# First modulation of a two-layer diffusion backbone: float32 products on four column groups, with tokens and context loaded first

## The chip, the cores and the metric

The kernel runs on one core of a Trainium2 chip. The metric is the device time of one execution in microseconds (us); lower is better. TensorE (PE) multiplies, ScalarE (ACT) and VectorE (DVE) work on elements, GpSimd (POOL) fills constants, and SyncE (SP) issues every transfer from device memory (HBM).

## The reference, cut to what matters

256 latent tokens `x` and 256 context tokens `ctx`, 2048 features each, pass two layers in float32. Ahead of each layer a conditioning vector gives shift, scale and gate vectors. The change concerns the first two of them (`sh1`, `sc1`) of layer 0, for tokens and context, and the first use of them, the queries' and keys' latents.

```python
for l in range(DEPTH):
    mod_x = (jax.nn.silu(c) @ w_mod[l] + b_mod[l])[:, None, :]      # c: (1, 2048), w_mod[l]: (2048, 12288)
    sh1, sc1, g1, sh2, sc2, g2 = jnp.split(mod_x, 6, axis=-1)
    hx = modulate(rmsnorm(x, norm1[l]), sh1, sc1)                   # h * (1 + scale) + shift
    if need_ctx:                                                    # layer 0
        mod_c = jax.nn.silu(c_ctx) @ w_mod[l] + b_mod[l]
        csh1, csc1, ... = jnp.split(mod_c, 6, axis=-1)
        hc = modulate(rmsnorm(ctx, norm1[l]), csh1, csc1)
    ...                                                             # layer 0: attention and pooling of
    x = x + g1 * yx                                                 # hx @ w_in, hc @ w_in; layer 1: Fourier
    x = x + g2 * sq_relu_mlp(modulate(rmsnorm(x, norm2[l]), sh2, sc2), w_mlp1[l], w_mlp2[l])
return rmsnorm(x, final_norm)
```

## The kernel before, in words

Features lie on the 128 partitions, in 16 blocks; tokens lie along the free axis. Weights come as tiles `W` of 128 x 2048 float32 (1 MB each) into a pool of seven buffers. `split` turns part of a tile into two float32r halves, H (a rounded copy, by ACT) and L (the rest, by DVE), and a product is then H times the activation's two halves plus L times its first.

The order on SP and PE is the order of the program text; DVE, ACT and POOL are ordered by the scheduler. A load waits for its buffer, and so for the last reader of the tile that held it. The other modulation vectors of both layers are products on DVE (`mod_step`), which are paced between later loads.

The stage that the change touches is the first one. `w_mod`'s shift and scale columns of layer 0 are 32 tiles: four groups `ng` of 512 features, for each first the scale (`which` 1) and then the shift (0), each in four tiles `kt`. A tile holds four blocks `kb` of 128 inputs by 512 features. `start_tile` multiplies it with the two conditioning vectors (tokens, context): a stationary operand of few useful columns, and the 512 features of the tile streaming past it, into a row tile `mrow` of one PSUM bank. The number `PLAIN[ng]` says how many of the four blocks are multiplied as float32 as they are (`cstf`, 32 stationary columns), and the others are split (`cst`, 128 columns of which four are used: the H and the L part of each vector). A float32 product is one instruction in the program and two passes on PE in the trace.

When the four tiles of a row are done, and one tile of the next row is through, `start_columns` copies the row to SBUF (ACT) and turns it into columns with four small products with `sel` (`mtr`), and DVE adds the bias. `latents(ng)` then loads `w_kv` and `w_q` for these four blocks of 128 features, makes `hc` and `hx` (`modulated`: DVE writes `xr`, ACT the first half of `h`, DVE the second), and does two half steps of products into the banks `ka` and `qa`. Its first half follows tile `LT[0]` of the next group's eight and its second half tile `LT[1]`, both counted from 0; the second half of the third group's and all of the fourth's come after the last tile. The tokens `x` are loaded after tile `LX` (5), the context `cx` after tile 7, and their sums of squares and the two normalizing rows follow at the tiles `NT` (8 and 9).

After this stage come pooling woven with attention (first products into `pu`), the output projection, the MLP, and layer 1.

Of the kernel before, what the change touches and what calls it, by code (L numbers as in the profile page):

```python
# [16 lines left out]
P = 128  # L17
# [10 lines left out]
WINDOWS = (2, 4, 8, 16)  # L28
PLAIN = (2, 1, 1, 0)
LATE = 2  # L30
LX, LC, NT, LT = 5, (7,), (8, 9), (2, 5)

# columns of the packed vectors
V_N1 = (0, 16)
# [10 lines left out]
def hybrid_dit(ctx: ExitStack, tc: tile.TileContext, xT, ctxT, c2, cb_in, vecs, wmod_s, wmod0, wmod1,  # L45
               w_q, w_kv, w_pl, w_uq, w_ukv, w_pool, w_oe, w_oo, w1, w2,
               rope, band, ident_in, sel_in, dftc, dftn, out):
    nc = tc.nc
    # the tensor engine and the loads go in the order of this text
    ctx.enter_context(tc.manual_schedule(engines={mybir.EngineType.SP, mybir.EngineType.PE}))  # L50
# [32 lines left out]

# [1 line left out]
    todo = []  # L85
# [26 lines left out]

# [1 line left out]
    def load(src, n=2048):  # L114
# [8 lines left out]
    def split(w, lo, n, nn):  # L123
        """n columns from lo of a tile, as [(H, L)] by row blocks of nn"""
        h = hp.tile([P, 1024], F32R, name="H", tag="H")
        l = hp.tile([P, 1024], F32R, name="L", tag="L")
        nc.scalar.copy(h[:, :n], w[:, lo:lo + n])  # L127
        nc.vector.tensor_tensor(l[:, :n], w[:, lo:lo + n], h.bitcast(F32)[:, :n], ALU.subtract)  # L128
        return [(h[:, i:i + nn], l[:, i:i + nn]) for i in range(0, n, nn)]
# [9 lines left out]
    def wide(ps, wts, j, acts, first, last):  # L139
        """a block of 128 output features in a bank: [HH | HL + LH]"""  # L140
        js = slice(j * P, (j + 1) * P)
        n = len(wts)
        for k, (h, l) in enumerate(wts):
            mm(ps, h[:, js], acts[k], first and k == 0, False)
            mm(ps[:, T:], l[:, js], acts[k][:, :T], False, last and k == n - 1)

    def narrow(o, wts, j, acts, first, last):
        """the same, summed in half a bank; first starts the bank"""
        js = slice(j * P, (j + 1) * P)
        n = len(wts)  # L150
        for k, (h, l) in enumerate(wts):
            mm(o, h[:, js], acts[k][:, :T], first and k == 0, False)
            mm(o, h[:, js], acts[k][:, T:], False, False)
            mm(o, l[:, js], acts[k][:, :T], False, last and k == n - 1)

    def plain(o, wts, j, acts, first, last):
        """the same in float32 as it is, for products too small to repay the splitting"""
        js = slice(j * P, (j + 1) * P)
# [4 lines left out]
    def linear(tiles, acts, evac, nb=4, slim=False, drain=False):  # L163
        """nb output blocks from [(sources of their tiles of four row blocks, first row block)];
        yields after each half of a tile; with drain the last tile goes block by block"""
        if slim:
# [4 lines left out]
        for i, (srcs, k0) in enumerate(tiles):  # L171
            for s, src in enumerate(srcs):
                w = load(src)
                final = i == len(tiles) - 1
                for k in (0, 2):
# [9 lines left out]
                    for j in range(4):  # L185
# [3 lines left out]
                        else:  # L189
                            wide(o, wts, j, part, first, last)  # L190
                        # a bank is read only when all of it is done
                        if last and not slim:
# [10 lines left out]
    def weave(main, filler):  # L203
        """main says how many steps of the filler come before its next one"""
        for n in main:
# [3 lines left out]

# [1 line left out]
    def sumsq(acc, src, first):  # L211
# [7 lines left out]
    def token_sums(ps, src, n, first, last, nb=2):  # L219
        """adds a block's sums over its features, by token, in columns of 128"""  # L220
        for b in range(nb):
            mm(ps[:, b:b + 1], src[:, b * P:(b + 1) * P], ones[n], first and b == 0, last and b == nb - 1)

    def rstd(ps, nb=2, first=False):
        """1/sqrt(mean + eps) by token"""
        v, s, r, a = (tiny(4, m)[:, :nb] for m in ("va", "sd", "rr", "nw"))
# [17 lines left out]
    def spread(r, nb=2):  # L244
        """those columns as rows, the same on each partition"""
        o = bank("rb")
# [14 lines left out]
    def scales(m, which, norm, lo=0, n=NB):  # L261
        """norm * (1 + scale), in place of the scale"""
        v = m[:, which, lo:lo + n]
# [6 lines left out]

# [1 line left out]
    c2s = cp.tile([P, 32], F32, name="c2s")  # L272
# [19 lines left out]

# [1 line left out]
    csil = cp.tile([P, 2, NB], F32, name="csil")  # L294
# [4 lines left out]
    nc.vector.tensor_copy(cstf[:, :, 1], csil[:, 1])  # L299
    cst = [ap.tile([P, 4, P], F32R, name=f"cst{i}", tag="a") for i in range(4)]  # L300
    for i in range(4):
        nc.gpsimd.memset(cst[i].bitcast(F32), 0.0)
        for s in range(2):
            nc.scalar.copy(cst[i][:, :, s], csil[:, s, 4 * i:4 * i + 4])
            nc.vector.tensor_tensor(cst[i][:, :, 2 + s], csil[:, s, 4 * i:4 * i + 4],
                                    cst[i].bitcast(F32)[:, :, s], ALU.subtract)

    def start_tile(row, ng, which, kt):
        """a tile's share of 512 features of shift (0) or scale (1), for the tokens and the context"""
        w = load(wmod_s[which * 4 + ng, kt])  # L310
        whole_ = PLAIN[ng]
        for lo in range(0, 4 - whole_, 2):
            n = min(2, 4 - whole_ - lo)
            for i, (h, l) in enumerate(split(w, lo * 512, n * 512, 512)):
                kb = lo + i
                mm(row, cst[kt][:, kb, :], h, kt == 0 and kb == 0, False)
                mm(row, cst[kt][:, kb, :], l, False, kt == 3 and kb == 3)
        for kb in range(4 - whole_, 4):
            mm(row[:32], cstf[:, 4 * kt + kb, :], w[:, kb * 512:(kb + 1) * 512], False, kt == 3 and kb == 3)

# [12 lines left out]

# [1 line left out]
    qa = [bank(f"qa{i}") for i in range(2)]  # L335
# [3 lines left out]
    def latents(ng):  # L339
# [5 lines left out]
        for i in range(2):  # L345
# [14 lines left out]
            yield  # L360

    columns = lat = None
    for ng in range(4):
        for which in (1, 0):
            row = bank("mrow")
            for kt in range(4):
                start_tile(row, ng, which, kt)
                if ng == 0 and which == 1 and kt == 0:
                    nc.sync.dma_start(vec, vecs)
                    nc.sync.dma_start(sel, sel_in)  # L370
                    nc.sync.dma_start(ident, ident_in)
                at = 8 * ng + 4 * (1 - which) + kt
                if at == LX:
                    for i in range(4):
                        nc.sync.dma_start(x[:, 4 * i:4 * i + 4], xT[:, 4 * i:4 * i + 4])
                    accs = [stat("accx"), stat("accc")]
                    for i in range(NB):
                        sumsq(accs[0], x[:, i], i == 0)
                if at in LC:
                    for i in range(8 // len(LC)):  # L380
                        cx.append(funit("cx").rearrange("p (a b) -> p a b", b=T))
                        i = len(cx) - 1
                        nc.sync.dma_start(cx[i], ctxT[:, 2 * i:2 * i + 2])
                        for i in (2 * i, 2 * i + 1):
                            sumsq(accs[1], cx[i // 2][:, i % 2], i == 0)
                if columns and kt == 0:
# [32 lines left out]

# [1 line left out]
    mixed = []  # L421

    def residual(l, which, stats, slim=False):
        """adds gate * product to the stream (and gathers its squares)"""
        def at(ng):
# [20 lines left out]
    def pooling():  # L446
        # by token, so that the centred means are products with a banded matrix
        us = [[bank(f"pu{tb}{hf}") for hf in range(2)] for tb in range(2)]
# [45 lines left out]

# [1 line left out]
    attn = []  # L496

    def rotary(s):
        """in place on [2 x 64, tokens]"""
        r = scr("rot")  # L500
# [5 lines left out]
    def attention():  # L506
# [35 lines left out]
        def project(pr):  # L542
            """a pair's heads: queries and keys by feature, values by token"""
            w = load(w_ukv[pr], 1024)
# [142 lines left out]

# [1 line left out]
    wc = load(dftc)  # L689
# [12 lines left out]
    def channels(g):  # L702
        """cosine and sine sums over a group's channels, by token"""
        st = []
# [22 lines left out]
    def positions(st):  # L727
        """the same over the tokens, by feature: blocks k, 128 + k and their mirrors"""
        def part(o, lo, which, first):
# [53 lines left out]
def _pack(w, nn=512, nk=4):  # L783
    """[K, N] in tiles [N / nn, K / (128 nk)] of [128, nk * nn], one run per partition"""
    k, n = w.shape
# [4 lines left out]
def _tables():  # L790
# [21 lines left out]
    sel = np.zeros((P, 2))  # L812
    sel[:4] = [[1, 0], [0, 1], [1, 0], [0, 1]]
    return [np.ascontiguousarray(t, dtype=np.float32) for t in (rope, band, np.eye(P), sel, dftc, dftn)]
# [51 lines left out]
```

## Time and profile before

| | |
|---|---|
| median of 3 runs | 2037.41 us (2036.52 to 2053.14) |
| span of the profiled execution | 2038.8 us |
| PE busy | 1993.2 us (98%) |
| DVE busy | 1508.1 us (74%) |
| ACT busy | 1067.7 us (52%) |
| moved from and to HBM | 537.68 MB, mean 264 GB/s |

The span runs from the first to the last instruction of one profiled execution. No separate time of that execution is listed beside its span, which lies 1.4 us above the median of the runs. Busy shares are means over stages with different limits, so the first stage is read by itself.

### The profile page before, as it was taken

To read this page: it belongs to the slowest core of one execution; us is meant where nothing else is said; L and a number is where in the kernel's file an instruction comes from. 1 tells how busy PE (TensorE), PEld (TensorE's weight loads), DVE (VectorE), ACT (ScalarE), POOL (GpSimd) and SP (SyncE) were. 2 spreads that over 40 slices of the span, in tenths; PEclk is the share of its full clock that TensorE was granted. 3 is DMA by queue.
4 is the path that set the end of the run, shared out by engine and by line. 5 is a ranking of instruction groups with operands and counts; after the bars stand their busy time and mean duration, and the time that the engine had idled before them with its cause. 6 is when DMAs were issued, how large, how long until landed. Compare 5 with 4: busy or idle time off the path is not lost.

```text
span 2038.8 us, 29093 instructions
## 1 busy us (share of the span) xinstructions
PE 1993.2 (98%) x11492; PEld 1712.8 (84%) x11492; DVE 1508.1 (74%) x2084; ACT 1067.7 (52%) x1715; POOL 2.9 (0%) x14
## 2 busy tenths in 40 slices
PE   6999999999999999999999999999999999999997
PEld 2678778988888888888888888888888888888887
DVE  5877868989888788888878677798555655655564
ACT  5564545355544554554555455556455545645563
POOL 0000000000000000000000000000000000000000
PEclk9999999989999999999999999999999999999998
DMA  9777888959988888887888516599555555555541
GB/s 387 266 303 297 328 305 321 374 180 392 343 330 331 328 310 327 318 321 295 344 319 325 217 62 230 183 347 375 189 190 196 181 194 188 184 199 194 186 145 42
DMA packets 77465, 537.68 MB, mean 264 GB/s; under 512 B 8848, under 2 KB 9104, under 8 KB 13968
## 3 DMA queue, kind: packets, MB, share of 16 engines
q1 hardware_dynamic: 77328, 535.82, 71.0%
q8 instruction: 90, 1.47, 0.3%
q14 instruction: 47, 0.39, 0.1%
HBM read 533.69 MB, written 2.10 MB: 263 GB/s over the span
## 4 chain that ended last, share of the span: by engine, by line
PE 96%; DMA 1%; DVE 1%; ACT 1%; issue 0%; SPq 0%; DVEq 0%; ACTq 0%
PE mm L82 80%; PE mrow L82 3%; PE pu L82 2%; PE ka L82 2%; PE sc L82 2%; DMA W<-in_wmod_s 1%; PE qa L82 1%; PE f L82 1%; PE pv L82 1%; PE qn L82 1%; PE v L82 1%; PE p L82 1%; PE kn L82 1%; PE rb L82 0%; PE var L82 0%; PE tr L607 0%
## 5 line engine op out<-in xcount | busy, mean ns | idle before, releaser
L128 DVE TENSOR_TENSOR L<-W,H 128x1024 fp32r<-128x1024 f32 (+2 forms) x668 | 795.4, 1207 | 390.6 <-ACT H L127 387.7
L127 ACT CAST H<-W 128x1024 fp32r<-128x1024 f32 (+2 forms) x668 | 685.5, 1037 | 605.1 <-PE mm L82 531.7
L82 PE MATMUL mm<-h,H 128*128 128x512 f32 x2048 | 720.7, 396 | 3.6 <-DVE h L258 3.6
L82 PE MATMUL mm<-hid,H 128*128 128x512 f32 (+1 forms) x2176 | 718.4, 382 | 0.0
L82 PE MATMUL mm<-h,L 128*128 128x256 f32 x2048 | 575.8, 281 | 0.0
L82 PE MATMUL mm<-hid,L 128*128 128x256 f32 x2048 | 574.6, 281 | 0.0
L82 PEld LDWEIGHTS mm<-hid,H 128*128 128x128 f32 x2176 | 399.8, 188 | 84.5
L82 PEld LDWEIGHTS mm<-h,H 128*128 128x128 f32 x2048 | 385.7, 188 | 94.7 <-issue 2.1
L82 PEld LDWEIGHTS mm<-h,L 128*128 128x128 f32 x2048 | 388.7, 190 | 0.0
L82 PEld LDWEIGHTS mm<-hid,L 128*128 128x128 f32 x2048 | 387.4, 189 | 0.0
L98 DVE SCALAR_TENSOR_TENSOR W<-W,cb 128x2048 f32<-128x2048 f32 x160 | 365.0, 2284 | 0.0
L433 DVE SCALAR_TENSOR_TENSOR x<-mm,mods,x 128x256 f32<-128x256 f32 x176 | 79.9, 479 | 43.8 <-PE mm L82 26.4
L82 PE MATMUL mm<-fr,H 128*128 128x512 f32 (+1 forms) x320 | 91.0, 352 | 0.0
L432 ACT ACTIVATE rt<-mm,mods 128x256 f32<-128x256 f32 x132 | 61.7, 469 | 52.4 <-PE mm L82 50.9
L666 ACT ACTIVATE rl<-g 128x256 f32<-128x256 f32 x128 | 53.2, 415 | 53.9 <-DVE g L664 53.3
L82 PE MATMUL mm<-fr,L 128*128 128x256 f32 x256 | 72.1, 281 | 0.0
L664 DVE TENSOR_TENSOR g<-mm,b 128x256 f32<-128x256 f32 x128 | 53.6, 419 | 20.0 <-ACT b L663 19.7
L663 ACT COPY b<-mm 128x256 f32<-128x256 f32 x128 | 45.7, 357 | 41.7 <-PE mm L82 41.7
L82 PEld LDWEIGHTS mm<-fr,H 128*128 128x128 f32 x320 | 55.8, 188 | 9.0
L667 ACT ACTIVATE hd<-rl 128x256 f32<-128x256 f32 x128 | 53.3, 416 | 2.7
L133 DVE TENSOR_TENSOR hid<-hd,hid 128x256 fp32r<-128x256 f32 x128 | 53.8, 420 | 0.4
L82 PE MATMUL mrow<-H,cst 128*128 128x512 f32 x96 | 41.5, 432 | 12.0 <-ACT H L127 12.0
(190 smaller groups left out, 1638.2 us busy)
## 6 DMA issues: line engine op xcount, KB each, us to landing
W<-in_w SPq DMA_DIRECT2D x256, 1024.0 KB, 5.2
W<-in_wmod SPq DMA_DIRECT2D x160, 1024.0 KB, 6.7
W<-in_wmod_s SPq DMA_DIRECT2D x32, 1024.0 KB, 7.3
W<-in_w_oe SPq DMA_DIRECT2D x16, 1024.0 KB, 7.8
W<-in_w_oo SPq DMA_DIRECT2D x16, 1024.0 KB, 4.9
W<-in_w_pl SPq DMA_DIRECT2D x8, 1024.0 KB, 6.3
W<-in_w_q SPq DMA_DIRECT2D x4, 1024.0 KB, 9.4
W<-in_w_kv SPq DMA_DIRECT2D x4, 768.0 KB, 10.2
```

The lines of the kernel that those rows point to most:

```text
L82: nc.tensor.matmul(o, l, r, start=start, stop=stop, skip_group_check=True)
L98: nc.vector.scalar_tensor_tensor(w, w, 1.0, cb, ALU.mult, ALU.mult, accum_out=mods[l][:, which, j:j + 1])
L127: nc.scalar.copy(h[:, :n], w[:, lo:lo + n])
L128: nc.vector.tensor_tensor(l[:, :n], w[:, lo:lo + n], h.bitcast(F32)[:, :n], ALU.subtract)
L133: nc.vector.tensor_tensor(u[:, n:2 * n], src, u.bitcast(F32)[:, :n], ALU.subtract)
L432: nc.scalar.mul(t, half(ps, 1), g)
L433: nc.vector.scalar_tensor_tensor(x[:, i], ps[:, :T], g, x[:, i], ALU.mult, ALU.add)
L663: nc.scalar.copy(b, half(ps, 1))
L664: nc.vector.tensor_tensor(s, half(ps, 0), b, ALU.add)
L666: nc.scalar.activation(r, s, AF.Relu)
L667: nc.scalar.square(f, r)
```

## The change

All four blocks of every modulation tile are multiplied as plain float32, with no splitting. Block `kb` goes into partitions 32 kb to 32 kb + 31 of the row's bank, that is through column group `kb` of the array, with its own 32 stationary columns and its own 512 streaming columns. `sel` now adds four partial rows per vector where it added two. The split vectors `cst` go. The tokens, the context and the three small tables are loaded ahead of the first modulation tile, and the sums of squares come first on ACT and DVE. `NT` goes from (8, 9) to (3, 5) and `LT` from (2, 5) to (1, 4). Comments are taken out.

```diff
-PLAIN = (2, 1, 1, 0)
 LATE = 2
-LX, LC, NT, LT = 5, (7,), (8, 9), (2, 5)
+NT, LT = (3, 5), (1, 4)
...
-    cst = [ap.tile([P, 4, P], F32R, name=f"cst{i}", tag="a") for i in range(4)]
-    for i in range(4):
-        nc.gpsimd.memset(cst[i].bitcast(F32), 0.0)
-        for s in range(2):
-            nc.scalar.copy(cst[i][:, :, s], csil[:, s, 4 * i:4 * i + 4])
-            nc.vector.tensor_tensor(cst[i][:, :, 2 + s], csil[:, s, 4 * i:4 * i + 4],
-                                    cst[i].bitcast(F32)[:, :, s], ALU.subtract)
 
     def start_tile(row, ng, which, kt):
...
         w = load(wmod_s[which * 4 + ng, kt])
-        whole_ = PLAIN[ng]
-        for lo in range(0, 4 - whole_, 2):
-            n = min(2, 4 - whole_ - lo)
-            for i, (h, l) in enumerate(split(w, lo * 512, n * 512, 512)):
-                kb = lo + i
-                mm(row, cst[kt][:, kb, :], h, kt == 0 and kb == 0, False)
-                mm(row, cst[kt][:, kb, :], l, False, kt == 3 and kb == 3)
-        for kb in range(4 - whole_, 4):
-            mm(row[:32], cstf[:, 4 * kt + kb, :], w[:, kb * 512:(kb + 1) * 512], False, kt == 3 and kb == 3)
+        for kb in range(4):
+            mm(row[32 * kb:32 * kb + 32], cstf[:, 4 * kt + kb, :], w[:, kb * 512:(kb + 1) * 512],
+               kt == 0, kt == 3)
...
+    accs = [stat("accx"), stat("accc")]
+    for i in range(0, NB, 4):
+        nc.sync.dma_start(x[:, i:i + 4], xT[:, i:i + 4])
+        for j in range(i, i + 4):
+            sumsq(accs[0], x[:, j], j == 0)
+    for i in range(0, NB, 2):
+        cx.append(funit("cx").rearrange("p (a b) -> p a b", b=T))
+        nc.sync.dma_start(cx[-1], ctxT[:, i:i + 2])
+        for j in range(2):
+            sumsq(accs[1], cx[-1][:, j], i + j == 0)
+    nc.sync.dma_start(vec, vecs)
+    nc.sync.dma_start(sel, sel_in)
+    nc.sync.dma_start(ident, ident_in)
     columns = lat = None
...
-    sel[:4] = [[1, 0], [0, 1], [1, 0], [0, 1]]
+    sel[0::32, 0] = sel[1::32, 1] = 1
```

The first place is the queue of loads on SP, from the start to the first weights of the latents. Before:

```order
L273 DMA c2s<-in_c 128x32
L116 DMA W<-in_wmod_s 128x2048
L369 DMA vec<-in_vecs 128x286
L370 DMA sel<-in_sel 128x2
L371 DMA ident<-in_ident 128x128
L116 DMA W<-in_wmod_s 128x2048 x5
L375 DMA x<-in_xT 128x1024 x4
L116 DMA W<-in_wmod_s 128x2048 x2
L383 DMA cx<-in_ctxT 128x512 x8
L116 DMA W<-in_wmod_s 128x2048 x3
L116 DMA W<-in_w_kv 128x1536
```

The same stretch of SP's queue after the change:

```order
L272 DMA c2s<-in_c 128x32
L351 DMA x<-in_xT 128x1024 x4
L356 DMA cx<-in_ctxT 128x512 x8
L359 DMA vec<-in_vecs 128x286
L360 DMA sel<-in_sel 128x2
L361 DMA ident<-in_ident 128x128
L115 DMA W<-in_wmod_s 128x2048 x10
L115 DMA W<-in_w_kv 128x1536
```

Everything that is not a modulation tile has moved ahead of the first one, and the first weights of the latents follow ten tiles instead of eleven.

The second place is PE where the second group's latents begin (`ka`). Before, the columns of the shift (`mtr_763`) stand two tiles further up, and the second of these tiles, with its three split blocks and one plain one, leads into the latents:

```order
L82 MATMUL mrow_743<-H_789,cst2_109 128x512
L82 MATMUL mrow_743<-L_790,cst2_109 128x512
L82 MATMUL mrow_743<-H_789,cst2_109 128x512
L82 MATMUL mrow_743<-L_790,cst2_109 128x512
L82 MATMUL mrow_743<-H_797,cst2_109 128x512
L82 MATMUL mrow_743<-L_798,cst2_109 128x512
L82 MATMUL mrow_743<-W_787,cstf_103 32x512
L82 MATMUL ka0_133<-h_808,H_848 128x256 x2
L82 MATMUL ka0_133<-h_808,L_849 128x256
```

After, the same columns (`mtr_592`) have one tile behind them, and a tile is four plain products:

```order
L81 MATMUL mrow_479<-W_577,cstf_103 32x512 x4
L81 MATMUL mrow_583<-W_584,cstf_103 32x512 x4
L81 MATMUL mtr_592<-sel_95,rows_590 128x2 x4
L81 MATMUL mrow_583<-W_599,cstf_103 32x512 x4
L81 MATMUL ka0_109<-h_609,H_649 128x256 x2
L81 MATMUL ka0_109<-h_609,L_650 128x256
```

PE comes to the latents' products one tile after the columns instead of two, and needs H and L of `w_kv` there.

The third place is DVE at the same point. Before, the second half of `w_kv`'s first piece (`L_849`) is made ahead of the shift's columns:

```order
L128 TENSOR_TENSOR L_849<-W_804,H_848 128x768
L330 TENSOR_TENSOR mods0_98<-mtr_763,vec_93 128x4
L330 TENSOR_TENSOR cmod_100<-mtr_763,vec_93 128x4
L258 SCALAR_TENSOR_TENSOR h_808<-xr_809,cmod_100,h_808 128x256
L258 SCALAR_TENSOR_TENSOR h_813<-xr_814,mods0_98,h_813 128x256
```

After, it (`L_650`) stands behind the columns and behind all eight `h`, and ACT has the same order with H (`H_649`):

```order
L317 TENSOR_TENSOR mods0_98<-mtr_592,vec_93 128x4
L317 TENSOR_TENSOR cmod_100<-mtr_592,vec_93 128x4
L257 SCALAR_TENSOR_TENSOR h_609<-xr_610,cmod_100,h_609 128x256
L257 SCALAR_TENSOR_TENSOR h_614<-xr_615,mods0_98,h_614 128x256
L257 SCALAR_TENSOR_TENSOR h_619<-xr_620,cmod_100,h_619 128x256
L257 SCALAR_TENSOR_TENSOR h_624<-xr_625,mods0_98,h_624 128x256
L257 SCALAR_TENSOR_TENSOR h_629<-xr_630,cmod_100,h_629 128x256
L257 SCALAR_TENSOR_TENSOR h_634<-xr_635,mods0_98,h_634 128x256
L257 SCALAR_TENSOR_TENSOR h_639<-xr_640,cmod_100,h_639 128x256
L257 SCALAR_TENSOR_TENSOR h_644<-xr_645,mods0_98,h_644 128x256
L127 TENSOR_TENSOR L_650<-W_605,H_649 128x768
```

The split of the latents' weights has moved behind the eight `h` of its group.

## Rows read from the trace of the kernel before

**Rows 1.** The page: busy time of TensorE, share of the span, instructions.

```profile
PE 1993.2 (98%) x11492; PEld 1712.8 (84%) x11492; DVE 1508.1 (74%) x2084; ACT 1067.7 (52%) x1715; POOL 2.9 (0%) x14
```

**Rows 2.** Stretches: start:end, us, busy time per engine, clock, DMA share, GB/s.

```profile
0.00:60.33 60.33, 43.16 (x121) 17.43 (x121) 33.79 (x80) 32.19 (x68) 2.85 (x14) 0.92 0.93 364
60.33:176.00 115.67, 114.72 (x711) 92.74 (x710) 92.08 (x143) 74.22 (x103) 0.00 (x0) 1.00 0.78 301
...
30.00:40.00 10.00, 4.24 (x7) 1.55 (x8) 8.54 (x18) 7.55 (x19) 0.00 (x0) 0.75 1.04 408
```

**Rows 3.** The chain that ended last: start us, us, what; start to 174 us.

```profile
15.25 15.03 DMA W<-in_wmod_s
30.30 4.68 DMA cx<-in_ctxT
...
76.75 4.50 PE ka L82 x36
81.26 2.88 PE qa L82 x24
84.14 7.50 PE mrow L82 x24
91.64 0.98 PE mtr L82 x8
...
139.54 3.65 PE mrow L82 x16
...
170.45 2.88 PE qa L82 x24
173.33 2.75 PE pu L82 x12
```

**Rows 4.** TensorE in order of time: start us, us, instruction, count.

```profile
18.12 1.90 PE L82 MATMUL mrow<-W,cstf 128*32 128x512 f32 x4
19.96 0.50 PE L82 MATMUL mrow<-H,cst 128*128 128x512 f32 x1
...
60.33 0.65 PE L82 MATMUL ka<-h,H 128*128 128x256 f32 x2
```

**Rows 5.** ScalarE in order of time: the first three modulation tiles as they land.

```profile
6.17 1.04 ACT L127 CAST H<-W 128x1024 fp32r<-128x1024 f32 x1 [2.47 <-DMA W<-in_wmod_s]
10.19 1.04 ACT L127 CAST H<-W 128x1024 fp32r<-128x1024 f32 x1 [2.97 <-DMA W<-in_wmod_s]
12.69 1.04 ACT L127 CAST H<-W 128x1024 fp32r<-128x1024 f32 x1 [1.46 <-DMA W<-in_wmod_s]
```

**Rows 6.** Transfers: issues, KB each, median us from issue to landing.

```profile
x<-in_xT SPq DMA_DIRECT2D x4, 512.0 KB, 15.3
cx<-in_ctxT SPq DMA_DIRECT2D x8, 256.0 KB, 9.9
```

**Rows 7.** VectorE and ScalarE in order of time: columns' addition, two `h`.

```profile
74.32 0.16 DVE L330 TENSOR_TENSOR mods<-mtr,vec 128x4 f32<-128x4 f32 x1 [1.07 <-PE mtr L82]
...
59.28 0.51 ACT L257 ACTIVATE h<-xr,cmod 128x256 fp32r<-128x256 f32 x1
59.69 0.49 ACT L257 ACTIVATE h<-xr,mods 128x256 fp32r<-128x256 f32 x1
```

**Rows 8.** Groups by form, first 180 us: count, busy us, mean ns, idle.

```profile
L128 DVE TENSOR_TENSOR L<-W,H 128x1024 fp32r<-128x1024 f32 x52 | 62.2, 1222 | 30.0 <-ACT H L127 30.0
...
L128 DVE TENSOR_TENSOR L<-W,H 128x768 fp32r<-128x768 f32 x8 | 7.6, 953 | 0.9 <-ACT H L127 0.9
L127 ACT CAST H<-W 128x768 fp32r<-128x768 f32 x8 | 6.7, 834 | 0.8 <-PE mrow L82 0.7
```

**Rows 9.** TensorE in order of time around its longest pause; idle before in brackets.

```profile
32.28 0.51 PE L82 MATMUL mrow<-H,cst 128*128 128x512 f32 x1 [2.48 <-ACT H L127]
36.27 0.80 PE L82 MATMUL mrow<-L,cst 128*128 128x512 f32 x1 [3.48 <-DVE L L128]
...
37.84 3.62 PE L82 MATMUL mrow<-W,cstf 128*32 128x512 f32 x4
```

More of the change, by code (lines that the diff above doesn't have):

```diff
@@ L367, in hybrid_dit @@
                 start_tile(row, ng, which, kt)
[L368 to L371, printed above, removed]
                 at = 8 * ng + 4 * (1 - which) + kt
[L373 to L385, printed above, removed]
                 if columns and kt == 0:
```

## The prediction

> **What bounds the kernel now.** I read the busy times first. PE is busy 98% of the span [rows 1], so only PE's own work and its pauses can change the time, and PE's pauses are almost all in one place. The stretches show it: up to 60.33 us, where the first latent product starts [rows 4], PE is busy 43.16 of 60.33 us while the DMA share is 0.93; from there to 176 us PE is busy 114.72 of 115.67 us at full clock and the DMA share is 0.78 [rows 2]. So the first stage has two halves: one bound by what lands and by the splitting on ACT and DVE, and one bound by PE. The chain says the same: transfers up to 35 us, then products without a gap to 173.33 us, where pooling takes over [rows 3]. Nothing behind 173.33 us is touched but the place of a few DVE and ACT instructions, so the gain is 173.33 us minus the new end of this stage.
>
> **Prices.** From the chain: half a latent step is 4.50 + 2.88 = 7.38 us and the columns are 0.98 us; a tile with one plain block is 7.50/3 = 2.50 us, a tile without one 3.65/2 = 1.83 us [rows 3]. A plain pass is (19.96 - 18.12)/4 = 0.46 us, switching included [rows 4]. A check of the recipe on the kernel before, from 60.33 us: 8 x 7.38 + 13 x 2.50 + 8 x 1.83 + 6 x 0.98 = 112.1 us against 113.0 us measured. What is missing, 0.9 us, is the uncovered copy of the last row and a first wait; I add 0.8 us for it below.
>
> **The first half, which is bound by DMA.** A tile lands every 12.69 - 10.19 = 2.50 us [rows 5]. Before, the first one is used at 6.17 us, so its data began at some 3.6 us; the next comes 4.02 us later, so the three small tables between them cost 1.5 us [rows 5]. Tokens and context are 4 x 512 + 8 x 256 KB [rows 6], four tiles' worth, 10.0 us. Loaded first, they put tile k at 3.6 + 10.0 + 1.5 + 2.5 (k + 1) us: 17.6 us for the first, 37.6 us for tile 8. The move is free by itself: the same bytes were ahead of the latents before, and PE only pauses earlier. The sums of squares that it brings forward run on ACT and DVE under these 17 us.
>
> **The splitting that goes** is large: of the 52 pieces of 1024 columns twelve belong to the latents and to pooling, the other 40 to the tiles, 40 x 1.22 = 49 us on DVE [rows 8], and as many on ACT. It pays only where PE waited for it, which is ahead of 60.33 us; the 3.48 us wait for L is one piece of that [rows 9].
>
> **What a tile costs PE now** is the open price: eight passes, two in each of four column groups. No products of different column groups stand in this trace. The bounds: if the groups do not overlap at all, 8 x 0.46 = 3.68 us; if all four run at once, 2 x 0.46 = 0.92 us. I take the middle. The trace shows passes of one product following each other on one group without overlap (four passes in 1.84 us [rows 4]), and PE's products starting in the order of the program everywhere. In that order the second pass of a block waits for its first, and the next block waits behind it; only then do they run side by side. So each group's second pass overlaps the next group's first: four pass lengths a tile, 1.84 us, and one more (0.46 us) for the first tile of each unbroken run. After the first latent step 22 tiles remain, in nine runs (broken by columns and latents): 22 x 1.84 + 9 x 0.46 = 44.6 us, against 47.1 us for 21 tiles before. That is the point of the forecast: two at a time, PE gains almost nothing per tile.
> The Trainium skill, "TensorE: Matmul & The Clock Gate", "The mechanism", says that products start and end strictly in program order; by that rule the tile comes to four pass lengths, and the starts in this trace agree, though none of them is on another column group.
>
> **The new wait.** The first latent half needs H and L of `w_kv`, which now stand behind the eight `h` of the group on ACT and DVE. After the columns on PE: two additions of 0.16 us, eight activations 0.41 us apart and the last one's 0.5 us [rows 7], then H 0.83 us and L 0.95 us [rows 8]: H at 4.5 us, L at 5.4 us. Before, the split stood ahead and two tiles (5.0 us) lay between; now one does. With a single tile of 2.3 us PE pauses 2.2 us for H and, after two products, 0.7 us for L: 2.9 us, twice (second and third group). The fourth group has 7.38 us of cover. Queued behind this wait on PE are the latents and every later tile, and with them the release of `W` buffers to SP. Such a pause also costs clock: over 30 to 40 us, with PE 42% busy, the granted clock is 0.75 [rows 2], and after pauses of 2.48 and 3.48 us four plain passes took 3.62 instead of 1.90 us [rows 4, 9], the 1.2 GHz level against 2.4. I put 1.3 us on each of three pauses, 4 us in all; bounds 0 and 7 us.
>
> **The sum.** Tile 8 lands at 37.6, PE 2.3 us, columns 0.98 us, H 4.5 us: the first latent product at 45.3 us instead of 60.33, with one tile less done. Then 0.9 (first wait for L) + 8 x 7.38 = 59.0 + 44.6 + 6 x 0.98 = 5.9 + 0.8 + 5.8 (waits) + 4 (clock) = 121.0 us: the stage ends at 166.3 us instead of 173.33, 7 us earlier. The execution read here has a span of 2038.8 us, 1.4 us above the median of 2037.41; I take the difference off the median: **2030 us**. With the clock's bounds, a scheduler's shuffle of some DVE and ACT work behind, and 1.7 to 2.2 us a tile, this case alone spans 2022 to 2038 us.
>
> **Rivals.**
> *All four groups at once.* If a waiting second pass does not hold back the next group, a tile is 0.92 us: 22 x 0.92 = 20.2 us, first product at 43.9 us, but waits of 4.2 us instead of 2.9 and some 5 us of clock: end at 43.9 + 0.9 + 59.0 + 20.2 + 5.9 + 0.8 + 8.4 + 5 = 144.1 us, 29 us earlier: **2008 us**. DMA allows it: up to the last latent weights there are some 44 tiles' worth, 110 + 5 = 115 us, and these weights are needed at 129 us. For it: two passes are separate instructions with weights of 32 columns, small enough to be loaded ahead. Against: the order of starts.
> The Trainium skill, "TensorEngine Tiling (Array Packing)", "Key Properties", says that different tiles of the array load and multiply in parallel; taken without the order of starts it gives this case, and no run here shows it yet.
> *The groups do not overlap* (the change does not do what it says), and it is slower. A tile is 3.68 us, above the 2.50 us of its landing, so PE is late from the start: 17.6 + 9 x 3.68 + 2 x 0.98 + 4.5 = 57.2 us, some 59 us with a slow start, for the first latent product, then 0.9 + 59.0 + 81 + 5.9 + 0.8 + 3 + 2: end at 212 us, 38 us later: **2076 us**. For it: passes on one group show no overlap. The sum turns to a loss from about 2.4 us a tile.
> *A partial overlap*, 2.4 to 3.3 us a tile, because four streams share what feeds the array, would give 2038 to 2062 us.
>
> **How the numbers follow.** Two at a time 0.47, all four 0.32, partial 0.06, none 0.15. A measurement of this kernel tells about 1% from no change, 2017 to 2058 us. Faster by over 1%: nearly all of the four-at-once case and a little of the forecast's best end, 0.33. Slower: the no-overlap case and a piece of the partial one, 0.17. Same: 0.50. The range takes in the four-at-once case and leaves out no overlap: 2003 to 2046 us.
>
> **What would show it.** In the profile after: first `ka` product near 45 us; starts of a tile's eight passes in pairs 0.44 to 0.46 us apart (all within 0.9 us for the four-at-once case, one after another for none); pauses of about 3 us ahead of the second and third groups' latents, ended by H and L; `pu` starting near 166 us; the stretches behind it as long as before. The forecast falls if the tile's length is not 1.8 to 2.0 us, and that one number decides between the cases.

## The result, and the profile after

The changed kernel takes 2013.23 us (median of 4, 1998.94 to 2014.13), the kernel before beside it 2045.28 us (median of 4, 2036.52 to 2053.58); the ratio on record is 0.986, interval 0.983 to 0.989 (the two medians alone would give 0.984). The time lies in the forecast's range, but the mechanism is not the forecast's: it is the rival in which all four column groups run at once (2008 us).

Executions of either kernel lie on steps some 14 us apart (before near 2025, 2037 and 2052 us, after near 1999 and 2013 us; the last section shows what differs between them), and from step to step, counted from the lowest, the change gives 24 to 26 us. I therefore compare kernels by landmarks in the first stage, above all by the start of the first `pu`, the first product behind the stage; the medians stand beside them.

The page after, its line of busy times, as [rows 1] before: PE is busy 43 us less, DVE 56.5 us less, ACT 50.3 us less.

```profile
PE 1950.2 (97%) x11492; PEld 1683.3 (84%) x11492; DVE 1451.6 (72%) x2020; ACT 1017.4 (51%) x1651; POOL 1.0 (0%) x10
```

The stretches after, as [rows 2] before (start:end, us, busy time of PE, PEld, DVE, ACT, POOL with counts, granted clock, DMA share, GB/s):

```profile
0.00:45.00 45.00, 20.44 (x112) 7.95 (x112) 21.79 (x68) 19.88 (x50) 1.00 (x10) 0.87 0.97 383
45.00:150.00 105.00, 95.73 (x719) 77.94 (x719) 45.65 (x90) 36.99 (x57) 0.00 (x0) 0.91 0.92 374
70.00:80.00 10.00, 6.42 (x35) 5.20 (x36) 7.69 (x14) 6.65 (x12) 0.00 (x0) 0.71 1.00 415
```

The second half of the stage was PE's before, at full clock and with a DMA share of 0.78. Now PE pauses in it, its clock falls, and the DMA share is 0.92: the work on PE has shrunk so far that the making of `h`, H and L shows through. Transfers do not yet: from 45.3 us to `pu` PE waits for none. The chain after, in the second group of features, and its last group's first half step, to lay beside [rows 3]:

```profile
66.34 3.57 PE mrow L81 x32
69.91 1.00 PE mtr L81 x8
...
71.19 3.30 ACT h L256 x8
74.50 0.73 ACT H L126
75.25 0.97 DVE L L127
76.26 6.44 PE ka L81 x34
...
85.58 2.71 PE mrow L81 x24
...
89.27 4.42 PE ka L81 x36
...
106.50 6.67 PE ka L81 x34
...
132.81 4.33 PE ka L81 x34
```

Four tiles take 3.57 us and three 2.71 us: 0.90 us a tile, against 2.50 and 1.83 before. A pause then stands in the chain, filled by ACT's eight `h`, H and L, and the half step of `ka` behind it takes 6.44 or 6.67 us where an undisturbed one takes 4.33 to 4.42. What slows it is the clock. Two stretches of 2 us in the second group's step, with the granted clock third from the end, show it: 11 products at 0.50, the 1.2 GHz level, against 19 at 1.00:

```profile
78.00:80.00 2.00, 2.00 (x11) 2.00 (x11) 1.43 (x2) 0.00 (x0) 0.00 (x0) 0.50 0.98 414
82.00:84.00 2.00, 2.00 (x19) 2.00 (x19) 0.00 (x0) 0.00 (x0) 0.00 (x0) 1.00 0.98 401
```

The same in order of time on PE, with the idle time ahead in brackets; first the tile ahead of the first latents, last the first `pu`:

```profile
41.45 1.06 PE L81 MATMUL mrow<-W,cstf 128*32 128x512 f32 x8 [0.44 <-DMA W<-in_wmod_s]
45.39 0.80 PE L81 MATMUL ka<-h,H 128*128 128x256 f32 x2 [2.88 <-ACT H L126]
...
75.27 0.79 PE L81 MATMUL ka<-h,H 128*128 128x256 f32 x2 [3.38 <-ACT H L126]
76.26 0.58 PE L81 MATMUL ka<-h,L 128*128 128x256 f32 x1 [0.20 <-DVE L L127]
...
147.06 0.40 PE L81 MATMUL pu<-H,h 128*128 128x512 f32 x1
```

The first latent product starts at 45.39 us instead of 60.33, and `pu` at 147.06 instead of 173.17 (the chain of [rows 3] has it from 173.33): 26 us earlier. The span is some 27 us shorter (2011.6 against 2038.8), so nearly all of the gain is made before `pu` and none of it is lost behind. Both of these executions have one MLP at either of the two speeds of the last section, so these cancel.

How does a tile come to 0.90 us? Each product of a column group has two passes, each with its own load of 32 columns. The starts show it at the head of the tiles in front of the first group's second half step: first what PE starts up to 55.72 us, then the weight loads up to 56.5 us:

```profile
55.27 0.64 PE L81 MATMUL mrow<-W,cstf 128*32 128x512 f32 x4
```

```profile
55.27 0.16 PEld L81 LDWEIGHTS mrow<-W,cstf 128*32 128x32 f32 x8
55.73 0.13 PEld L81 LDWEIGHTS mrow<-W,cstf 128*32 128x32 f32 x4 [0.30 <-issue]
56.16 0.13 PEld L81 LDWEIGHTS mrow<-W,cstf 128*32 128x32 f32 x4 [0.30 <-issue]
```

Four passes start at 55.27 us within 0.02 us of each other, one in each column group; the loads, eight at first and then four by four, 0.43 us apart, show the next passes coming in fours too. Both passes of block 0 belong to one instruction, which stands ahead of block 1's in the program; its second pass does not hold block 1 back.

### The profile page after: what moved, and what is told of

Its sections match the earlier page's. It is cut to its first block, busy times and chain, and to the rows that moved or that the text cites. A ratio compares the mean times of both kernels' runs of the same rounds, so it can differ in the third digit from the quotient of the medians.

```text
span 2011.6 us, 28859 instructions
## 1 busy us (share of the span) xinstructions
PE 1950.2 (97%) x11492; PEld 1683.3 (84%) x11492; DVE 1451.6 (72%) x2020; ACT 1017.4 (51%) x1651; POOL 1.0 (0%) x10
## 4 chain that ended last, share of the span: by engine, by line
PE 95%; ACT 2%; DVE 1%; DMA 1%; issue 0%; SPq 0%; DVEq 0%; ACTq 0%
PE mm L81 81%; PE pu L81 2%; PE ka L81 2%; PE sc L81 2%; PE mrow L81 1%; PE f L81 1%; PE qa L81 1%; PE pv L81 1%; ACT h L256 1%; PE qn L81 1%; DMA W<-in_wmod_s 1%; PE v L81 1%; PE p L81 1%; PE kn L81 1%; PE mtr L81 0%; PE var L81 0%
## 5 line engine op out<-in xcount | busy, mean ns | idle before, releaser
L127 DVE TENSOR_TENSOR L<-W,H 128x1024 fp32r<-128x1024 f32 (+1 forms) x612 | 737.7, 1220 | 371.1 <-ACT H L126 369.9
L126 ACT CAST H<-W 128x1024 fp32r<-128x1024 f32 (+1 forms) x612 | 634.8, 1046 | 570.3 <-PE mm L81 545.5
L81 PE MATMUL mrow<-W,cstf 128*32 128x512 f32 x256 | 35.0, 668 | 22.1 <-DVE accc L216 19.1
```

Source lines behind the costliest of these rows:

```text
L81: nc.tensor.matmul(o, l, r, start=start, stop=stop, skip_group_check=True)
```

## The experiments

Medians are followed by the number of executions; ratios are against the kernel before on the same chip (for one_group to lt_2_5 a median of 2037.18 us of 13, for the last three 2037.62 us of 23, for after the 2045.28 us in the table).

| kernel | first `ka`, us | first `pu`, us | first `kn`, us | median, us | ratio, interval |
|---|---|---|---|---|---|
| before | 60.33 | 173.17 | 194.73 | 2045.28 (4) | 1 |
| after | 45.39 | 147.06 | 168.49 | 2013.23 (4) | 0.986, 0.983 to 0.989 |
| one_group | 59.93 | 201.61 | 222.97 | 2075.01 (4) | 1.018, 1.012 to 1.024 |
| two_in_pairs | 45.78 | 162.70 | 183.05 | 2027.11 (8) | 0.996, 0.993 to 0.999 |
| split_ahead | 45.09 | 134.63 | 159.34 | 2004.46 (4) | 0.983, 0.978 to 0.988 |
| lt_2_5 | 47.15 | 141.95 | 163.93 | 2003.61 (4) | 0.986, 0.979 to 0.992 |
| loads_late | 49.26 | 151.94 | 173.35 | 2011.21 (10) | 0.990, 0.985 to 0.994 |
| loads_only | 63.09 | 178.37 | 198.51 | 2043.62 (10) | 1.003, 1.000 to 1.006 |
| ahead_mods_late | 45.20 | 135.43 | 155.21 | 2006.85 (6) | 0.985, 0.979 to 0.990 |

The landmarks are starts of the first product of each tile in the profiled execution; `kn` is the first product behind the norms of the latents.

### one_group: the same products, all through one column group

```diff
-            mm(row[32 * kb:32 * kb + 32], cstf[:, 4 * kt + kb, :], w[:, kb * 512:(kb + 1) * 512],
-               kt == 0, kt == 3)
+            g = 0
+            mm(row[32 * g:32 * g + 32], cstf[:, 4 * kt + kb, :], w[:, kb * 512:(kb + 1) * 512],
+               kt == 0 and kb == 0, kt == 3 and kb == 3)
```

The four blocks add up in 32 partitions, and only these are copied and turned.

> Same loads, same order, all four plain products of a tile in column group 0 (only 32 rows are copied and turned). Theory (the four groups run at once and that is what pays): eight passes follow each other, 8 x 0.44 = 3.5 us a tile and about 3.6 with switching instead of 0.90; 22 tiles behind the first latent product then cost 59 us more, the pauses ahead of the latents shrink by 2 to 3 us each, and the first latent product comes some 14 us later: slower than the changed kernel by 58 to 70 us, 2070 to 2082 us, and slower than the kernel before by 1.5 to 2%. Rival (what pays is the splitting that ACT and DVE no longer do, and PE has room): within 15 us of the changed kernel, faster than before.

Its chain, at the second group:

```profile
86.16 13.85 PE mrow L81 x32
```

Four tiles take 13.85 us, 3.46 us each, 3.9 times the 0.89 us of four groups; `pu` comes 28 us later than before, and the kernel is slower than before by 1.8%, as expected (2070 to 2082 us). So neither the missing splits nor the early loads pay for plain products: the overlap does.

### two_in_pairs: two column groups, two blocks in each

```diff
-            mm(row[32 * kb:32 * kb + 32], cstf[:, 4 * kt + kb, :], w[:, kb * 512:(kb + 1) * 512],
-               kt == 0, kt == 3)
+            g = kb // 2
+            mm(row[32 * g:32 * g + 32], cstf[:, 4 * kt + kb, :], w[:, kb * 512:(kb + 1) * 512],
+               kt == 0 and kb % 2 == 0, kt == 3 and kb % 2 == 1)
```

Blocks 0 and 1 go through group 0, then blocks 2 and 3 through group 1. Ahead of group 1's first pass four passes of group 0 stand in the program. If starts keep the order of the program, the two groups hardly overlap; if each group has a line of its own, they overlap fully.

> Two column groups, in the order 0, 0, 1, 1: four passes in a row on one group, then four on the other. Theory (each group has its own queue, a waiting pass does not hold back the other group): first starts of both groups within some 0.02 us, a tile takes four pass lengths, 4 x 0.43 = 1.75 us, about 18 us slower than the changed kernel, 2030 us. Rival (program order with a look ahead of one waiting pass or so): the second group starts only near the end of the first one's four passes, seven pass lengths or 2.6 to 3.1 us a tile, 40 to 50 us slower than the changed kernel, 2052 to 2065 us.

What PE starts at the head of a tile, up to 69.5 us, and then the weight loads up to 70.3 us:

```profile
69.07 0.63 PE L81 MATMUL mrow<-W,cstf 128*32 128x512 f32 x2
```

```profile
69.07 0.15 PEld L81 LDWEIGHTS mrow<-W,cstf 128*32 128x32 f32 x4
69.53 0.12 PEld L81 LDWEIGHTS mrow<-W,cstf 128*32 128x32 f32 x2 [0.31 <-issue]
69.96 0.12 PEld L81 LDWEIGHTS mrow<-W,cstf 128*32 128x32 f32 x2 [0.31 <-issue]
```

And its chain there:

```profile
69.14 7.01 PE mrow L81 x32
```

Two products start at 69.07 us, one in each group, although a second product of group 0 stands between them in the program. Behind the first four the loads come in pairs, 0.43 to 0.46 us apart, and a tile takes 7.01/4 = 1.75 us, half of one_group's 3.46. A column group whose passes wait, three of them here, does not hold back the next group. Whether each group has a line of its own or the engine looks past three waiting passes, this run can't tell. `pu` starts at 162.70 us.

### split_ahead: the first split of `w_kv` ahead of the eight `h`

```diff
     def latents(ng):
...
+        first = split(wkv, 0, 768, 384)
+        behind.extend(made)
         for k in range(4 * ng, 4 * ng + 4):
...
-            for n, (h, l) in enumerate(split(wkv, 768 * i, 768, 384)):
+            for n, (h, l) in enumerate(split(wkv, 768 * i, 768, 384) if i else first):
```

Every `h` of the group is ordered behind this split on ACT and DVE (`behind`), so H and L come ahead of the `h` again, as before.

> The changed kernel with the first split of each group's w_kv queued on ACT and DVE ahead of that group's eight h. Theory (the new wait costs its pauses and the half clock that follows them): each of the three pauses of 3.6 to 4.4 us shrinks to 1 us or less and the latent half step behind it takes 7.4 us instead of 9 to 9.5, so 8 to 16 us faster than the changed kernel, 1997 to 2006 us. Rival (the loads bound this stage anyway, its DMA share is 0.92 to 0.97): pauses move to the modulation tiles or to the first weights of pooling, under 4 us faster.

Its chain up to the second group, in the third, and behind the stage:

```profile
27.89 15.88 DMA W<-in_w_kv
...
72.19 4.49 PE ka L81 x35
...
101.81 8.41 DMA W<-in_wmod_s
...
142.95 2.19 DVE W L98 x2
```

PE in order of time at the first group, and between `pu` and `kn`:

```profile
45.09 0.58 PE L81 MATMUL ka<-h,H 128*128 128x256 f32 x1 [3.14 <-ACT h L260]
...
148.25 1.50 PE L81 MATMUL rb<-dg,one 128*128 128x128 f32 x8 [2.32 <-DVE dg L249]
```

The stretch from 45 to 150 us there, to lay beside the same stretch of after:

```profile
45.00:150.00 105.00, 99.67 (x768) 80.70 (x768) 55.11 (x117) 41.17 (x68) 0.00 (x0) 0.96 0.98 396
```

The second group's half step starts 4 us earlier and takes 4.49 us instead of 6.44: pause and slow products go together. `pu` comes 12.4 us earlier than after. The first group's pause does not shrink to 1 us or less as expected: it is 3.14 us, against 2.88 in after, since every `h` there now stands behind the split of `w_kv`, which lands at 43.77 us. So the next limit there is a transfer. Later one of modulation tiles stands in the chain for 8.41 us, and the DMA share is 0.98, but between 45 and 135 us PE itself waits only 0.7 us for a tile. From `pu` to `kn` 24.7 us pass instead of 21.4: PE waits 2.32 us for `dg`, a step of the norms, and in the chain paced modulation products on DVE (`W` of line 98) stand ahead of it. The median is 9 us below that of after; the two intervals overlap.

### lt_2_5: the latents one tile later

```diff
-NT, LT = (3, 5), (1, 4)
+NT, LT = (3, 5), (2, 5)
```

> The changed kernel with LT (2, 5) as before: one more tile of cover ahead of the latents. Theory: each of three pauses is shorter by one tile, 0.9 us, the work is the same, so 2 to 3 us faster or, with the pause still over 2 us and the same loss of clock, no change that can be measured. Rival (the earlier latents pay, since PE has nothing else to do): 3 to 6 us slower.

PE in order of time at the second group:

```profile
71.61 1.92 PE L81 MATMUL mrow<-W,cstf 128*32 128x512 f32 x16
...
76.07 0.51 PE L81 MATMUL ka<-h,H 128*128 128x256 f32 x2 [2.53 <-ACT H L126]
77.06 0.38 PE L81 MATMUL ka<-h,L 128*128 128x256 f32 x1 [0.49 <-DVE L L127]
```

Its chain there, and the stretch of 70 to 80 us (granted clock third from the end):

```profile
77.06 4.33 PE ka L81 x34
```

```profile
70.00:80.00 10.00, 6.98 (x58) 4.62 (x51) 7.46 (x14) 7.17 (x13) 0.00 (x0) 1.00 1.01 411
```

`pu` comes 5.1 us earlier than after; I had expected 2 to 3 us. The pause itself is only 0.6 us shorter (2.53 + 0.49 instead of 3.38 + 0.20), but the clock stays at 1.00 where it was 0.71, and the half step is 2.1 us shorter; with the third group's (4.34 instead of 6.67) that makes some 5.6 us, of which the first latent product takes part back: it comes 1.8 us later, with one tile of 0.90 us more done. What I had left out was the clock.

### loads_late: tokens, context and tables back in their old places

```diff
-NT, LT = (3, 5), (1, 4)
+LX, LC, NT, LT = 5, (7,), (8, 9), (1, 4)
```

The loads and the sums of squares stand again behind the sixth and eighth tile (`LX`, `LC`), as in the kernel before; the rest is as after.

> The changed kernel with tokens, context and tables loaded where the kernel before has them (after tiles 0, 5 and 7) and NT (8, 9); products on four groups and LT (1, 4) stay. Theory (the place of the loads is free, the products pay): the same bytes are ahead of the first latents, so the first latent product comes at 45 to 48 us and the first pooling product at 147 to 151 us; 0 to 4 us slower than the changed kernel. Rival (it is loading first that pays, since the 32 sums of squares then run before ACT and DVE are needed): first latent product at 55 us or later, 10 to 15 us slower than the changed kernel.

The first latent product comes 3.9 us later than after, at 49.26, `pu` 4.9 us later: about one microsecond beyond the expected stretches. The norms of tokens and context are now late, as its chain shows just ahead of the first half step:

```profile
45.73 2.02 PE rb L81 x8
...
48.18 1.28 DVE xr L255 x3
49.46 0.41 DVE h L257
49.91 6.90 PE ka L81 x35
```

So of the 26 us the place of the loads is worth 5, and the products on four column groups 21, in this order of taking apart. The 21 hold the third part of the change too, `LT` of (1, 4), which by itself costs 5.1 us (lt_2_5).

### loads_only: the kernel before with the loads first

```diff
-LX, LC, NT, LT = 5, (7,), (8, 9), (2, 5)
+NT, LT = (3, 5), (2, 5)
...
+    for i in range(0, NB, 4):
+        nc.sync.dma_start(x[:, i:i + 4], xT[:, i:i + 4])
...
```

The other half alone: split products as before, loads and sums of squares ahead of the first tile.

> The kernel before, split products and LT (2, 5) as they are, with tokens, context and tables loaded first and NT (3, 5). Theory: the waits for H and L behind the sums of squares go (some 10 us of PE pauses ahead of 60 us), but PE starts 11 us later and then needs 2.5 to 3.0 us a tile, so the first latent product comes at 54 to 58 us instead of 60.33 and the rest is as before: 2 to 6 us faster than the kernel before. Rival (the load order carries half of the gain or more): 12 us or more faster.

Both theories missed: `ka` and `pu` come 3 and 5 us later than before, and the time is 0.3% higher. What ACT does with the first tile, and its chain:

```profile
19.11 1.04 ACT L127 CAST H<-W 128x1024 fp32r<-128x1024 f32 x1 [1.42 <-DMA W<-in_wmod_s]
```

```profile
21.39 1.23 DVE L L128
22.67 13.31 PE mrow L82 x31
...
47.97 8.29 PE mrow L82 x24
```

PE has done a single product by 22.67 us; from there the chain is almost all PE, at 8.29/3 = 2.76 us a tile in the row shown. Before, PE worked on tiles while they landed [rows 4, 5]; here that work is pushed together behind the loads and lies bare. After, the same early pause costs little, since a tile of 0.90 us is done faster than the next one lands (2.50 us [rows 5]). The sums of squares explain little of the late start: the first tile itself is there only at 19.11 us, and DVE, busy with the sums, makes L at 21.39 us, 1.2 us after H is done.

### ahead_mods_late: split_ahead with DVE's paced products behind the norms

```diff
-    pace[0] = 1.6
+    pace[0] = 0.0
...
         kvh, kvl, ql = [], [], []
+        pace[0] = 1.75
```

> The changed kernel with the first split of each group's w_kv ahead of its eight h, and with the paced modulation products on DVE started only once the latents' norms are issued (pace 0 until then, 1.75 after, where it was 1.6). Theory: between the first pooling product and the first key product the order of DVE cost 24.7 us with the split ahead against 21.4 in the changed kernel; two modulation products of 2.3 us stand ahead of the norms there; without them that stretch takes 19 to 22 us, and the kernel is 2 to 5 us faster than with the split ahead alone, 1999 to 2003 us. Rival (the stretch waits for the loads of pooling's weights, since the stage before now takes all of the DMA): no change against the split ahead alone.

From `pu` to `kn` it takes 19.8 us instead of 24.7, as expected, and `kn` is at 155.21, 4.1 us earlier than in split_ahead. The time shows none of it, and the 1999 to 2003 us expected are missed: 2006.85 us against 2004.46, with intervals that overlap. PE's waits for DVE between 155 and 404 us, first a row of split_ahead, then two of this kernel (us in total, times, longest):

```profile
PE rb L81 <- DVE dg L249: 1.5, 1, 1.5
```

```profile
PE mm L81 <- DVE L L128: 4.6, 2, 4.2
PE rb L81 <- DVE dg L249: 2.0, 1, 2.0
```

The wait for L is new: DVE's products, moved back, now stand ahead of a split that PE needs. The 4 us are given back there, and more: PE's 2000th product starts at 353.8 us, 4.1 us earlier than in split_ahead, its 2200th at 384.4 us, 2.5 us later.

## Why the prediction was right in its range and wrong in its mechanism

**What bounds the kernel** held. PE was the limit from 60 us on, and the gain is what the stage ends earlier: 26 us at `pu`, some 27 us in the span. That the time lies in the range is owed to the rival that was taken into it: the forecast's own case reached from 2022 to 2038 us only.

**The first half** held in its parts, but that 45.3 us meets the measured 45.39 is luck. With the tile's real price the sum gives the rival's 43.9 us; the tiles land later by about as much, the tenth at 41.45 us (it ends PE's wait there) where the sum has 40.1. In the chain after, the columns of the second group's shift end at 70.91 us, H at 75.23 and L at 76.22: 4.3 and 5.3 us where I had 4.5 and 5.4. That the loads' move is "free by itself" is not what the runs show: without the faster tiles the first latent product comes 3 us later for it (loads_only), with them 4 us earlier (against loads_late).

**The splitting** that went is 56.5 us on DVE and 50.3 on ACT, differences of the pages' totals, where I had 49 on each. The sum left out sixteen pieces of 512 columns, 11.0 us on DVE and 9.8 on ACT in the trace before, and put ACT's piece of 1024 at DVE's 1.22 us, where it takes 1.04 [rows 5].

**The price of a tile** is the step that failed. I put 1.84 us, because "the second pass of a block waits for its first, and the next block waits behind it". It is 0.90 us, the rival's 0.92. The second pass does wait for its first, but the next block does not wait behind it if it goes through another column group: two_in_pairs shows it with four passes ahead in the program, one_group shows that the same products on one group take 3.46 us. From one group to two and to four the tile's time halves each time (3.46, 1.75, 0.89 us), so nothing shows of the partial overlap either. The starts in the trace before, on which I leaned, had no two products on different column groups, so they could not speak on this; I had noted that and still gave the rival less than the forecast.
The Trainium skill, "TensorE: Matmul & The Clock Gate", "The mechanism", says that products start and end strictly in program order; the starts in two_in_pairs (both groups at 69.07 us) differ from it, and the measurement decides. The Trainium skill, "TensorEngine Tiling (Array Packing)", "Key Properties", says that tiles of the array work in parallel; 3.46 us against 0.89 us agrees.

**The rest of the sum** can be tried apart from that price, since two_in_pairs is a kernel whose tile takes what I had forecast, 1.75 to 1.77 us. It starts `ka` at 45.78 and `pu` at 162.70 us, and takes 2027 us; the forecast for 1.84 us was 45.3, 166.3 and 2030. For after, the rival's sum gave 43.9, 144.1 and 2008; measured were 45.39, 147.06 and 2013.

**Waits and clock** were in the right place and somewhat small. Ahead of the second and third groups PE waits 3.38 + 0.20 us (2.9 in the forecast, 4.2 in the rival's sum), ended by H and then L as foretold. The three half steps behind a pause take 6.08, 6.44 and 6.67 us; against 4.42 that is 1.7 + 2.0 + 2.3 = 6.0 us for the clock, where I had 4 with bounds of 0 and 7. The fourth group's wait is 0.4 us (10.0 us in all, less 2.88 + 3.38 + 3.38):

```profile
PE ka L81 <- ACT H L126: 10.0, 4, 3.4
```

Together these two costs are the part of the change that can be taken back: split_ahead and lt_2_5 each remove some of it. Both end `pu` earlier than after by 12.4 and 5.1 us, and medians of 2004 us are 10 us below the 2013 us of after; with few executions and steps of 14 us the intervals against after overlap, so the landmarks carry this finding, not the medians.

**Slower** did not come about. one_group, where the groups cannot overlap, tries its prices: a tile takes 3.46 us (3.68 in the sum), the first latent product comes at 59.93 us (59), `pu` at 201.61 (212). That its median of 2075 us meets the 2076 is luck: `pu` is 10 us early, and two of its four executions lie on the slowest step, at 2081 us and more.

## What to carry to other kernels

Small float32 products whose stationary operand has few columns can be spread over the column groups of the array: the groups then work side by side, here 3.9 times as fast, even when passes of one group wait, and the splitting that made such products cheap on PE is no longer needed. When PE's share of a stage shrinks like this, look at what it waits for next: here splits queued behind other work on ACT and DVE, a pause that also costs the clock behind it, and once that is gone the transfer of `w_kv`. And measure an order of starts on the form of instruction in question before a forecast leans on it.

## What the runs showed of the hardware that I had not expected

**A waiting pass of one column group does not hold back another group.** Four plain products start within 0.02 us of each other, and the next passes 0.45 us later; with two groups the second one's first product starts with the first one's (69.07 us), although a whole product of the first group, which has to wait, stands between them in the program.

**A long stretch of products has two speeds at one granted clock.** In the multiplications of the two layers' MLPs PE is busy all the time, at granted clock 1.00, and still does either about 568 or about 579 products in 100 us. Two such stretches of the kernel before, then the same two of after:

```profile
500.00:600.00 100.00, 100.00 (x568) 86.75 (x567) 85.70 (x102) 47.72 (x77) 0.00 (x0) 1.00 0.90 351
1500.00:1600.00 100.00, 100.00 (x578) 88.17 (x578) 55.10 (x68) 58.40 (x101) 0.00 (x0) 1.00 0.56 190
```

```profile
500.00:600.00 100.00, 100.00 (x579) 87.46 (x578) 83.78 (x103) 50.09 (x70) 0.00 (x0) 1.00 0.86 327
1500.00:1600.00 100.00, 100.00 (x568) 86.67 (x567) 57.01 (x75) 55.63 (x90) 0.00 (x0) 1.00 0.53 182
```

The two speeds are 1.9% apart, which over an MLP stage of some 720 us is 14 us, as much as the steps between executions. Which layer has which speed differs between the profiled executions, with either DMA share. Both layers are fast in that of lt_2_5, the fastest of its four (1995.80 us), both slow in those of two_in_pairs and one_group, the slowest of their eight and four (2042.02 and 2081.94 us), and the other kernels' have one of each. What sets the speed was not tried and stays open. In a comparison where 1% matters it has to be taken out, by landmarks or by comparing executions of the same step.
